# A two-layer hybrid encoder on one core: sums, rows and value projections of the first phase placed differently, more fill ahead of the attention, and the weights' low halves subtracted by GpSimd in that phase

## The chip, the cores and the metric

One NeuronCore of a Trainium2 chip runs the whole kernel. The metric is device time in microseconds (us), the median of three runs. The engines are TensorE (PE in the profile; PEld is its weight load), VectorE (DVE), ScalarE (ACT), GpSimd (POOL) and SyncE (SP, which issues most DMAs). Each engine works through its own instructions in the order in which they were written, and waits on semaphores where it needs another engine's result.

## The reference, cut to what matters

```python
D_MODEL, SEQ, DEPTH, HEAD_DIM = 1024, 512, 2, 64          # batch 1, float32

for l in range(DEPTH):
    hn = rmsnorm(x, norm_mix_g[l])
    proj = hn @ w_in[l]
    (aq, ak, av, bx, by, cq, ck, cv, dq, dk, dv, gl) = jnp.split(proj, split_points, axis=-1)
    ya = mixer_a(aq, ak, av, ...)   # dense attention, 8 query and 2 key heads, q and k normed per head, axial rotary
    yb = mixer_b(bx, by, ...)       # width-4 convolution, two gated linear scans (forward, backward), GeLU gate
    yc = mixer_c(cq, ck, cv, ...)   # attention in a window of +-128, with a sink, rotary
    yd = mixer_d(dq, dk, dv, ...)   # three dilated windows, combined by their softmax denominators, rotary
    gates = sigmoid(gl + gate_bias[l])
    merged = sum(gates[:, :, n] * (y_n @ w_proj_n[l]) for n, y_n in enumerate((ya, yb, yc, yd)))
    x = x + merged @ w_out[l]
    hn = rmsnorm(x, norm_mlp_g[l])
    x = x + square(relu(hn @ w_mlp1[l])) @ w_mlp2[l]
return rmsnorm(x, norm_final_g)
```

## The kernel before, in words

**Weights.** All weights are cut into tiles of 128 x 1024 float32, 158 for each layer, in the order of `PLAN`. A tile is loaded by SP into `raw` (three buffers), ScalarE casts it to a high half `whi` (`whi()`, line 118), and VectorE subtracts: `wlo = raw - whi` (`wlo()`, line 127). Activations are split in the same way (`xh`, `xl`). A float32 product is then three matmuls in the fp32r type: xh by whi, xl by whi, xh by wlo (`mm3`, lines 177 to 179). A group of 128 output channels over all 512 positions takes one tile and 24 matmuls of 512 columns. `ahead` keeps the casts up to three tiles in front of the tile in use, and `lows` puts the subtractions behind each group in VectorE's order.

**First phase** (`phase1`, once a layer). It makes the projections for the mixers, 30 groups in the order of `P1SEQ`: BX and BY (mixer B), K (keys of A and C), AQ, CQ, DQ, DK. Six PSUM banks (tags mm, s, t, two each) take the groups in turn, and one bank, `misc`, takes small sums. Between the groups stand: the column norm (`norm_cols`), its row form (`norm_row`: four small matmuls against the identity, then `bcast_row`: a float32 matmul of a one-row operand with a row of ones, to spread the row over 128 partitions), the sums of squares for the per-head norms (`head_scale`), and a second row of three entries spread through a selector (line 484). `rope` turns pairs of groups: four VectorE products from PSUM (`tt`, line 338), sums (`stk`, `stkf`), and stores to DRAM by SP. Mixer B's element work waits in a queue of closures, `bq`, and `tick` runs some of them behind each group, as `TICKS` says.

**Behind it.** `values_ac` computes the values for A and C: four tiles of 128 positions, 24 matmuls of 256 columns each. Then attention A runs, step by step, mixed with `fill(1)`: the gate logits (GL) and the projection (PR) of mixer B, in pieces of 6 matmuls. `merge(a, b, na, nb, first)` starts with one attention step, then `first` pieces of fill, then spreads the rest in the ratio nb to na. `MG` holds these numbers for A, C and D. `attn_gqa` loads K and Q from DRAM at its start (lines 779, 783); its first two matmuls are lines 796 and 797. Attention C runs mixed with `values_d` (values for D, tiles VD) and more fill; attention D with fill; and `attn_d_end`, which combines the three dilated groups (weights `w12`, spread by the matmuls of line 1100), runs mixed with `FN` pieces of the last fill, with `E1`, `E2` and `E3` empty steps in it. Then come the output projection and the MLP.

Of the kernel before, what the change touches and what calls it, by code (L numbers as in the profile page):

```python
# [40 lines left out]
MG = ((35, 48, 3), (41, 71, 2), (18, 47, 12))  # L41

E1, E2, E3, FN = (1, 5, 2, 15)
# [32 lines left out]
class Body:  # L76
    RAWB, HLB = 3, 3

    def __init__(self, ctx, tc, w, x, vec, tab, cst, out):
        self.tc, self.nc, self.ctx = tc, tc.nc, ctx  # L80
        self.w, self.x, self.vec, self.tab, self.cst, self.out = w, x, vec, tab, cst, out
        pool = lambda n, b=1, **k: ctx.enter_context(tc.tile_pool(name=n, bufs=b, reuse_waits="tile", **k))
        self.cp = pool("cp")
        self.rawp, self.hlp = pool("rawp", self.RAWB), pool("hlp", self.HLB)
        self.xgp = pool("xgp")
        self.sm = pool("sm", 3)
        self.psp = pool("psp", 2, space=PSUM)
# [5 lines left out]
        self.rr = self.held = 0  # L93

# [27 lines left out]
    def wlo(self):  # L122
# [3 lines left out]
        for s in self.parts(i):  # L126
            self.nc.vector.tensor_tensor(out=lo[:, s], in0=raw[:, s], in1=hi[:, s].bitcast(F32), op=ALU.subtract)  # L127
# [45 lines left out]
    def mm3(self, ps, st, mv, n, step=0):  # L173
        mm = self.nc.tensor.matmul
        for k in range(n):
# [4 lines left out]
            if step and k % step == step - 1 and k < n - 1:  # L180
                yield
        self.lows()
# [78 lines left out]
    def norm_row(self, rcol, pool):  # L261
        nc = self.nc
        ps = self.misc()
        for c in range(4):
            nc.tensor.matmul(ps[0:1, c * 128:(c + 1) * 128], rcol[:, c:c + 1], self.ident)
        row = pool.tile([1, S], F32, tag="nrow", name="nrow", bufs=1)
        nc.scalar.copy(row, ps[0:1, :])
        return row

    def bcast_row(self, row, out):  # L270
        nc = self.nc
        ps = self.misc()
        nc.tensor.matmul(ps, self.ones[0:1, :], row)
        nc.scalar.copy(out, ps)
# [110 lines left out]
    def group(self, *key):  # L385
# [4 lines left out]
        self.run(self.proj8(hl, ps))  # L390
# [6 lines left out]
    def phase1(self, l):  # L397
# [15 lines left out]
        self.vD = self.drp.tile([3, S, 256], F32, tag="vD", name="vD")  # L413
        ckp, skp = self.table(4, "b0"), self.table(5, "b1")
        c1, s1 = self.table(0, "c1"), self.table(1, "s1")
        X, sqt = {}, {}
# [3 lines left out]
        def squares(key, Xs, n=128):  # L420
            sqt[key] = []
            for x in Xs:
                sq = p1.tile([128, S], F32, tag="sqq", name="sqq", bufs=2)
                ns.activation(out=sq[0:n], in_=x[0:n], func=AF.Square)
                sqt[key].append(sq)

        def head_scale(key, nh, sel, n=128):

            ps = self.misc()
            for c in range(4):  # L430
                for z in range(2):
# [12 lines left out]
        def q_scale(p):  # L444
            nv.tensor_tensor(
                out=self.rqs[:, :, 4 * p:4 * p + 4], in0=head_scale(p, 4, C_SEL4),
# [3 lines left out]

        X["bx", 0], X["bx", 1] = self.several([("BX", f) for f in range(2)], self.xmv, (1, 2, 3, 4, 6))
# [6 lines left out]
        row = self.norm_row(rcol, p1)  # L458
        X["k", 1] = self.group("K", 1)
        self.bcast_row(row, self.rb)  # L460
# [4 lines left out]
        nc.sync.dma_start(out=rd.rearrange("(o n) -> o n", o=1), in_=row)  # L465
# [6 lines left out]
        yk = head_scale("k", 2, C_SELK, 64)  # L472
# [4 lines left out]
        ps = self.misc()  # L477
        for c in range(4):
            nc.tensor.matmul(ps[0:3, c * 128:(c + 1) * 128], kc[:, c, :], self.ident)
        krow = p1.tile([3, S], F32, tag="krow", name="krow", bufs=1)  # L480
        ns.copy(krow, ps[0:3, :])
# [10 lines left out]
        q_scale(0)  # L492
# [5 lines left out]
        self.gelu_b(0, self.group("BY", 0))  # L498
        q10 = self.group("AQ", 1, 0)
# [3 lines left out]
        q_scale(1)  # L503
        self.rope(q10, q11, T, self.qsA[4:8], True)
        self.gelu_b(2, self.group("BY", 2))
        self.gelu_b(3, self.group("BY", 3))
# [5 lines left out]
        for n, (k, a) in enumerate(QKS):  # L512
# [8 lines left out]
            else:  # L521
                isq = k == "DQ"
                self.rope(x[0], x[1], seq if isq else key, (self.qD if isq else self.kD)[a], False, perm=a > 0)
        self.tick(100)
        nv.tensor_scalar(out=self.rs8p, in0=self.roff, scalar1=0.125, scalar2=None, op0=ALU.mult)

    def values_ac(self):
# [3 lines left out]
        for c in range(4):  # L531
# [10 lines left out]
            )  # L542
    def conv_b(self, l, f, ps):
# [124 lines left out]
    def values_d(self):  # L668
# [462 lines left out]
    def merge(self, a, b, na, nb, first=0):  # L1131
# [8 lines left out]
        step(0)  # L1140
        for _ in range(first):
            step(1)
# [10 lines left out]
    def layer(self, l):  # L1153
# [311 lines left out]
def _tables():  # L1465
# [52 lines left out]
```

## Time and profile before

| what | value |
|---|---|
| median of three runs | 2015.62 us (2018.54, 2015.62, 2010.84) |
| profiled execution, its own time | 2011.35 us |
| its span, first to last instruction | 2009.6 us |
| TensorE busy | 1988.3 us, 99% |
| weight loads busy | 1657.4 us, 82% |
| VectorE busy | 1300.8 us, 65% |
| ScalarE busy | 998.2 us, 50% |
| GpSimd busy | 0.2 us |
| granted TensorE clock, mean | 0.997 |

The time of the profiled execution is 1.75 us longer than its span. A matmul's duration in the profile is longer than its share of the pipeline: a matmul of 512 columns is listed with 0.39 us, but the next starts 0.23 us later, so the pace is read from one start to the next. For the same reason a busy share of 99% says only that TensorE was hardly ever without a matmul in flight.

### The profile page before, as it was taken

How to read it: one execution, taken by the hardware profiler on the slowest of the kernel's cores; microseconds unless marked ns; L12 is line 12 of the kernel's file. 1: busy time of each engine (PE TensorE's matmuls, PEld its weight loads, DVE VectorE, ACT ScalarE, POOL GpSimd, SP SyncE). 2: the span in 40 equal slices, each digit the busy share in tenths (PEclk: the TensorE clock that was granted, in tenths of full speed). 3: DMA queues.
4: the chain of work that ended last, by engine and by line, in shares of the span. 5: the costliest groups of instructions: out<-in, count | busy, mean ns of one | idle time of the engine just before them, and what ended most of it. 6: DMA issues, size and time to landing. Idle time of an engine off the chain costs nothing.

```text
span 2009.6 us, 26003 instructions
## 1 busy us (share of the span) xinstructions
PE 1988.3 (99%) x9752; PEld 1657.4 (82%) x9752; DVE 1300.8 (65%) x2322; ACT 998.2 (50%) x1749; POOL 0.2 (0%) x4
## 2 busy tenths in 40 slices
PE   9999999999999999999999999999999999999998
PEld 7888789888788888888878878898877888888887
DVE  6889775766666544444658897758676655544445
ACT  4357786855734332332323668868566344322322
POOL 0000000000000000000000000000000000000000
PEclk9999999999999999999999999999999999999999
DMA  5454424333443323333335553152353433323231
GB/s 192 145 159 137 131 65 144 116 103 118 114 133 130 95 95 95 105 95 95 134 99 166 157 156 106 44 177 95 105 134 95 163 95 97 103 95 99 91 104 63
DMA packets 91858, 233.35 MB, mean 116 GB/s; under 512 B 16442, under 2 KB 22714, under 8 KB 91732
## 3 DMA queue, kind: packets, MB, share of 16 engines
q1 hardware_dynamic: 88852, 227.49, 36.5%
q10 hardware_dynamic: 2880, 4.20, 0.6%
q8 instruction: 77, 1.26, 0.3%
q14 instruction: 49, 0.40, 0.1%
HBM read 207.38 MB, written 24.27 MB: 115 GB/s over the span
## 4 chain that ended last, share of the span: by engine, by line
PE 93%; DVE 3%; ACT 2%; DMA 1%; issue 1%; SPq 0%; DVEq 0%; ACTq 0%
PE ps_mm L177 14%; PE ps_mm L178 14%; PE ps_mm L179 14%; PE ps_t L177 6%; PE ps_t L179 6%; PE ps_t L178 6%; PE ps_s L177 6%; PE ps_s L178 6%; PE ps_s L179 6%; PE ps_o L856 2%; PE ps_t L835 2%; PE ps_s L796 1%; PE ps_s L797 1%; PE ps_s L946 1%; PE ps_o L1031 1%; PE ps_t L1005 1%
## 5 line engine op out<-in xcount | busy, mean ns | idle before, releaser
L118 ACT CAST whi<-raw 128x1024 fp32r<-128x1024 f32 (+1 forms) x318 | 329.1, 1041 | 302.6 <-PE ps_mm L178 94.1
L127 DVE TENSOR_TENSOR wlo<-raw,whi 128x1024 fp32r<-128x1024 f32 (+1 forms) x318 | 384.7, 1213 | 95.4 <-ACT whi L118 92.5
L177 PE MATMUL ps_mm<-xh,whi 128*128 128x512 f32 x720 | 286.3, 398 | 0.0
L179 PE MATMUL ps_mm<-xh,wlo 128*128 128x512 f32 x720 | 281.7, 391 | 0.0
L178 PE MATMUL ps_mm<-xl,whi 128*128 128x512 f32 x720 | 281.6, 391 | 0.0
L179 PEld LDWEIGHTS ps_mm<-xh,wlo 128*128 128x128 f32 x720 | 135.6, 188 | 29.7
L177 PEld LDWEIGHTS ps_mm<-xh,whi 128*128 128x128 f32 x720 | 135.7, 188 | 27.3 <-issue 0.8
L178 PEld LDWEIGHTS ps_mm<-xl,whi 128*128 128x128 f32 x720 | 135.7, 188 | 26.5
L177 PE MATMUL ps_t<-xh,whi 128*128 128x512 f32 x368 | 143.6, 390 | 0.0
L179 PE MATMUL ps_t<-xh,wlo 128*128 128x512 f32 x368 | 143.3, 389 | 0.3 <-DVE wlo L127 0.3
L178 PE MATMUL ps_t<-xl,whi 128*128 128x512 f32 x368 | 143.2, 389 | 0.0
L177 PE MATMUL ps_s<-xh,whi 128*128 128x512 f32 x352 | 138.5, 394 | 0.0
L179 PE MATMUL ps_s<-xh,wlo 128*128 128x512 f32 x352 | 137.0, 389 | 0.0
L178 PE MATMUL ps_s<-xl,whi 128*128 128x512 f32 x352 | 137.0, 389 | 0.0
L845 DVE TENSOR_TENSOR PT<-ps_t,PT 128x512 fp32r<-128x512 f32 (+2 forms) x128 | 75.1, 586 | 64.0 <-ACT PT L842 59.3
L829 ACT ACTIVATE P<-P,al 128x512 f32<-128x512 f32 (+2 forms) x128 | 82.6, 645 | 16.9 <-DVE al L828 15.7
L842 ACT CAST PT<-ps_t 128x512 fp32r<-128x512 f32 (+2 forms) x128 | 63.8, 500 | 46.7 <-PE ps_o L856 43.2
L177 PEld LDWEIGHTS ps_t<-xh,whi 128*128 128x128 f32 x368 | 69.1, 188 | 17.2 <-issue 3.0
L179 PEld LDWEIGHTS ps_t<-xh,wlo 128*128 128x128 f32 x368 | 69.1, 188 | 15.1 <-DVE wlo L127 0.7
L178 PEld LDWEIGHTS ps_t<-xl,whi 128*128 128x128 f32 x368 | 69.1, 188 | 14.3
L177 PEld LDWEIGHTS ps_s<-xh,whi 128*128 128x128 f32 x352 | 66.1, 188 | 14.8 <-issue 1.4
L178 PEld LDWEIGHTS ps_s<-xl,whi 128*128 128x128 f32 x352 | 66.1, 188 | 14.0 <-issue 0.5
(425 smaller groups left out, 4237.1 us busy)
## 6 DMA issues: line engine op xcount, KB each, us to landing
raw<-in_w_dram SPq DMA_DIRECT2D x314, 512.0 KB, 3.5
Qr<-qD SPq DMA_DIRECT2D x48, 128.0 KB, 3.9
Kd<-kD SPq DMA_DIRECT2D x48, 128.0 KB, 4.0
qsA<-stk SPq DMA_DIRECT2D x32, 128.0 KB, 2.3
qsC<-stk SPq DMA_DIRECT2D x32, 128.0 KB, 2.4
K<-ks SPq DMA_DIRECT2D x16, 256.0 KB, 5.9
Q<-qsA SPq DMA_DIRECT2D x16, 256.0 KB, 4.0
Q<-qsC SPq DMA_DIRECT2D x16, 256.0 KB, 5.2
```

What stands on the lines that cost most here:

```text
L118: self.nc.scalar.copy(hi[:, s], self.raws[i][:, s])
L127: self.nc.vector.tensor_tensor(out=lo[:, s], in0=raw[:, s], in1=hi[:, s].bitcast(F32), op=ALU.subtract)
L177: mm(ps, sh, mh, start=(k == 0), stop=False)
L178: mm(ps, sh, ml, start=False, stop=False)
L179: mm(ps, sl, mh, start=False, stop=(k == n - 1))
L796: nc.tensor.matmul(ps[:, 0:n], qq, Kt[j][:, 0, b0 * 128:b1 * 128], start=True, stop=False)
L797: nc.tensor.matmul(ps[:, 0:n], qq, Kt[j][:, 1, b0 * 128:b1 * 128], start=False, stop=True)
L829: ns.activation(out=P[:, 0:n], in_=P[:, 0:n], func=AF.Copy, scale=ls)
L835: nc.tensor.transpose(pt[:, b * 128:(b + 1) * 128], P[:, b * 128:(b + 1) * 128], self.ident)
L842: ns.copy(st["dst"][0], st["src"])
L845: nv.tensor_tensor(out=st["dst"][1], in0=st["src"], in1=st["dst"][0].bitcast(F32), op=ALU.subtract)
L856: nc.tensor.matmul(o, a, b, start=(n_ == 0), stop=(n_ == len(mm) - 1))
```

## The change

In the first phase (up to the AC values) the subtraction that gives `wlo` is issued to GpSimd; elsewhere it stays on VectorE. The two spread rows are now split in a high part (rows 0 on) and a low part (rows 32 on) and spread by one fp32r matmul each, with a selector built by memsets on GpSimd and a ScalarE copy. The key sums stack both halves of 64 partitions in one tile, so each position block takes one matmul instead of two. Sums and rows are issued inside groups (`within`), behind the fifth of eight steps. `values_ac` moves from the start of attention A to the end of the first phase, before the remaining closures, two of which now run behind each of its four parts. `merge` gets a place (`before`) for the first attention step among the first pieces of fill. `values_d` uses an order of matmuls that needs `wlo` last. `E1` and `FN` go up by one.

```diff
-MG = ((35, 48, 3), (41, 71, 2), (18, 47, 12))
-E1, E2, E3, FN = (1, 5, 2, 15)
+MG = ((35, 48, 5, 4), (41, 71, 2), (18, 47, 12))
+E1, E2, E3, FN = (2, 5, 2, 16)
...
     def wlo(self):
...
-            self.nc.vector.tensor_tensor(out=lo[:, s], in0=raw[:, s], in1=hi[:, s].bitcast(F32), op=ALU.subtract)
+            self.lo_engine.tensor_tensor(out=lo[:, s], in0=raw[:, s], in1=hi[:, s].bitcast(F32), op=ALU.subtract)
...
+    def mm3s(self, ps, st, mv, n, step=0):
+        mm = self.nc.tensor.matmul
+        for k in range(n):
+            (sh, sl), mh = st(k), mv(k)[0]
+            mm(ps, sh, mh, start=(k == 0), stop=False)
+            mm(ps, sl, mh, start=False, stop=False)
+            if step and 4 * k == 3 * n - 4:
+                yield
+        for k in range(n):
+            mm(ps, st(k)[0], mv(k)[1], start=False, stop=(k == n - 1))
+        self.lows()
...
-    def norm_row(self, rcol, pool):
+    def rows(self, cols, n, pool):
+        nc, rw = self.nc, self.rw
+        nc.vector.tensor_copy(rw[:, :, 0:n].bitcast(F32R), cols)
+        nc.vector.tensor_tensor(out=rw[:, :, 32:32 + n], in0=cols, in1=rw[:, :, 0:n], op=ALU.subtract)
         ps = self.misc()
+        m = 32 + n
         for c in range(4):
-            nc.tensor.matmul(ps[0:1, c * 128:(c + 1) * 128], rcol[:, c:c + 1], self.ident)
-        row = pool.tile([1, S], F32, tag="nrow", name="nrow", bufs=1)
-        nc.scalar.copy(row, ps[0:1, :])
+            nc.tensor.matmul(ps[0:m, c * 128:(c + 1) * 128], rw[:, c, 0:m], self.ident)
+        row = pool.tile([m, S], F32R, tag=f"row{n}", name="row", bufs=1)
+        nc.scalar.copy(row, ps[0:m, :])
         return row
-    def bcast_row(self, row, out):
+    def spread_rows(self, row, n, sel):
         ps = self.misc()
-        nc.tensor.matmul(ps, self.ones[0:1, :], row)
-        nc.scalar.copy(out, ps)
+        self.nc.tensor.matmul(ps, self.sel[0:32 + n, sel], row)
+        return ps
...
     def group(self, *key, within=None):
...
-        self.run(self.proj8(hl, ps))
+        for k, _ in enumerate(self.proj8(hl, ps, 1)):
+            if k == 4 and within:
+                within()
...
+        def head_sums(key, nh, sel, c0=0, c1=4):
+            if c0 == 0:
+                SUM[key] = self.misc()
+            sq = sqt[key]
+            for c in range(c0, c1):
+                for z, t in enumerate(sq):
                     nc.tensor.matmul(
-                        ps[:, nh * c:nh * c + nh], sqt[key][z][0:n, c * 128:(c + 1) * 128],
-                        self.cs[0:n, sel:sel + nh], start=(z == 0), stop=(z == 1),
+                        SUM[key][:, nh * c:nh * c + nh], t[:, c * 128:(c + 1) * 128],
+                        self.cs[:, sel:sel + nh], start=(z == 0), stop=(z == len(sq) - 1),
                     )
...
+        self.lo_engine = nc.gpsimd
...
-        X["q", 1] = self.group("AQ", 0, 1)
-        F = self.misc()
-        nc.tensor.matmul(F, self.cs[0:3, C_SEL3:C_SEL3 + 128], krow)
+        X["q", 1] = self.group("AQ", 0, 1, within=lambda: X.update(row=self.rows(kc, 3, p1)))
+        F = self.spread_rows(X["row"], 3, 1)
...
+        self.lo_engine = nc.vector
+        self.values_ac()
         self.tick(100)
...
+            self.tick(2)
...
-                yield from self.paced(last, self.mm3(
+                yield from self.paced(last, self.mm3s(
...
-        step(0)
-        for _ in range(first):
-            step(1)
+        for i in range(first + 1):
+            if i == before:
+                step(0)
+            if i < first:
+                step(1)
```

Three places show what stands where now. The first is TensorE's order where attention A of layer 0 begins: lines 177 to 179 (178 to 180 in the change) on `ps_t` of 256 columns are the last values, lines 796 and 797 (833 and 834) are the first attention step, and `ps_mm` of 512 columns is fill. Before:

```order
L177 MATMUL ps_t<-whi,xh 128x256
L178 MATMUL ps_t<-wlo,xh 128x256
L179 MATMUL ps_t<-whi,xl 128x256
L796 MATMUL ps_s<-K,Q 128x512 [waits DMAHW2_49,DMAHW3_49,DMAHW1_49,DVE_49]
L797 MATMUL ps_s<-K,Q 128x512
L177 MATMUL ps_mm<-xh,whi 128x512 [waits DVE_49,Activation_49]
L178 MATMUL ps_mm<-xl,whi 128x512
```

and now, after the 24 matmuls of the first fill group, of which the last two stand here:

```order
L179 MATMUL ps_mm<-xl,whi 128x512
L180 MATMUL ps_mm<-xh,wlo 128x512
L833 MATMUL ps_s<-K,Q 128x512 [waits DMAHW4_49,DMAHW3_49,DMAHW2_49]
L834 MATMUL ps_s<-K,Q 128x512
L178 MATMUL ps_mm<-xh,whi 128x512 [waits DVE_49,Activation_49]
L179 MATMUL ps_mm<-xl,whi 128x512
L180 MATMUL ps_mm<-xh,wlo 128x512 [waits DVE_49]
L178 MATMUL ps_mm<-xh,whi 128x512
L179 MATMUL ps_mm<-xl,whi 128x512
L180 MATMUL ps_mm<-xh,wlo 128x512
L833 MATMUL ps_s<-K,Q 128x512 [waits PE_49]
```

The first attention step has moved behind 24 matmuls of fill, and the second fill group now begins directly behind it.

The second place is ScalarE's order at the same point: `yB` is mixer B's last product, `VV` the AC values, `whi` the casts for the fill groups behind the first, and `P,al` the exponentials of the first attention step. Before:

```order
L653 CAST yB<-btq 128x512 [waits DVE_49]
L538 ACTIVATE VV<-ps_t,ny 128x4x64 [waits PE_49]
L538 ACTIVATE VV<-ps_mm,ny 128x4x64 [waits PE_49]
L538 ACTIVATE VV<-ps_s,ny 128x4x64 [waits PE_49]
L538 ACTIVATE VV<-ps_t,ny 128x4x64 [waits PE_49]
L118 CAST whi<-raw 128x1024 [waits DMAHW3_49]
L118 CAST whi<-raw 128x1024 [waits DMAHW4_49]
L808 ACT_TABLE_LOAD [waits DMAHW2_49,DMAHW1_49,DMAHW7_49,DMAHW0_49]
L808 ACTIVATE P,al<-ps_s,an,rqs 128x512 [waits DVE_49]
```

and now:

```order
L678 ACTIVATE btq<-btq 128x512 [waits DVE_49] x2
L573 ACTIVATE VV<-ps_s,ny 128x4x64 [waits PE_49]
L573 ACTIVATE VV<-ps_t,ny 128x4x64 [waits PE_49]
L690 CAST yB<-btq 128x512 [waits DVE_49]
L119 CAST whi<-raw 128x1024 [waits DMAHW3_49,Pool_49]
L119 CAST whi<-raw 128x1024 [waits DMAHW4_49,Pool_49]
L119 CAST whi<-raw 128x1024 [waits DMAHW1_49,PE_49,Pool_49]
L757 ACT_TABLE_LOAD
L757 ACTIVATE gt<-gt,d_hb 128x512 [waits DVE_49]
L845 ACTIVATE P,al<-ps_s,an,rqs 128x512 [waits DVE_49]
```

The values are read out among mixer B's closures now, and the casts still stand behind the last of those; a third cast and a gate have come in front of the first exponentials.

The third place is VectorE's order at the rotation of the last query pair of layer 0. Before:

```order
L338 TENSOR_TENSOR tt<-ps_s,s_210 128x512
L127 TENSOR_TENSOR wlo<-raw,whi 128x1024 [waits DMAHW4_49,Activation_49]
L361 TENSOR_TENSOR stkf<-tt 128x512 [waits DMAHW3_49,DMAHW5_49,DMAHW2_49,DVE_49]
L361 TENSOR_TENSOR stkf<-tt 128x512 [waits DVE_49]
L656 TENSOR_TENSOR yB<-btq,yB 128x512
L127 TENSOR_TENSOR wlo<-raw,whi 128x1024 [waits DMAHW5_49,PE_49,Activation_49]
```

and now:

```order
L356 TENSOR_TENSOR tt<-ps_t,c_215 128x512
L356 TENSOR_TENSOR tt<-ps_s,s_217 128x512
L379 TENSOR_TENSOR stkf<-tt 128x512 [waits DMAHW4_49,DMAHW3_49,DMAHW5_49,DMAHW2_49,DVE_49]
L379 TENSOR_TENSOR stkf<-tt 128x512 [waits DVE_49]
L693 TENSOR_TENSOR yB<-btq,yB 128x512 [waits Activation_49]
```

The subtractions are gone from VectorE's order; GpSimd has 33 of them in each layer, one behind the other, with nothing else between them.

## Rows read from the trace of the kernel before

**Rows 1.** The page's first part: busy us, share of the span, instructions.

```profile
PE 1988.3 (99%) x9752; PEld 1657.4 (82%) x9752; DVE 1300.8 (65%) x2322; ACT 998.2 (50%) x1749; POOL 0.2 (0%) x4
```

**Rows 2.** Waits of TensorE: engine, line, releaser, total us, times, longest us.

```profile
PE ps_s L796 <- DMA Q<-qsA: 5.4, 2, 3.2
...
PE ps_misc L1100 <- DVE w L1096: 2.0, 2, 1.0
...
PE ps_mm L178 <- DVE wlo L127: 1.3, 2, 0.6
```

**Rows 3.** TensorE's timeline where attention A begins, both layers (start us, us, instruction).

```profile
205.39 0.28 PE L179 MATMUL ps_t<-whi,xl 128*128 128x256 f32 x1
207.87 0.47 PE L796 MATMUL ps_s<-K,Q 128*128 128x512 f32 x1 [2.20 <-DMA Q<-qsA]
...
1198.58 0.28 PE L179 MATMUL ps_t<-whi,xl 128*128 128x256 f32 x1
1202.03 0.47 PE L796 MATMUL ps_s<-K,Q 128*128 128x512 f32 x1 [3.17 <-DMA Q<-qsA]
```

**Rows 4.** Windows after that wait in layer 1: busy us, PEclk behind POOL.

```profile
1203.40:1206.90 3.50, 3.50 (x11) 2.68 (x10) 3.46 (x7) 3.47 (x4) 0.00 (x0) 0.51 1.03 263
```

**Rows 5.** TensorE's timeline: first matmuls of two groups in succession.

```profile
67.03 0.39 PE L177 MATMUL ps_s<-xh,whi 128*128 128x512 f32 x1
...
72.47 0.39 PE L177 MATMUL ps_t<-xh,whi 128*128 128x512 f32 x1
```

**Rows 6.** ScalarE's and VectorE's timelines where attention A of layer 0 begins.

```profile
210.11 2.01 ACT L118 CAST whi<-raw 128x1024 fp32r<-128x1024 f32 x2
213.43 0.78 ACT L808 ACTIVATE P<-ps_s,an,rqs 128x512 f32<-128x512 f32 x1
...
198.42 2.13 DVE L361 TENSOR_TENSOR stkf<-tt 128x512 f32<-128x512 f32 x2
```

**Rows 7.** Timelines at the D values of layer 0: TensorE, then ScalarE.

```profile
333.02 0.28 PE L177 MATMUL ps_mm<-whi,xh 128*128 128x256 f32 x1
333.93 0.39 PE L178 MATMUL ps_mm<-wlo,xh 128*128 128x256 f32 x1 [0.64 <-DVE wlo L127]
...
331.59 1.98 ACT L118 CAST whi<-raw 128x1024 fp32r<-128x1024 f32 x2
```

**Rows 8.** Timelines at the end of attention D, layer 0: VectorE, then TensorE.

```profile
572.87 0.69 DVE L159 TENSOR_TENSOR yD<-og,yD 128x512 fp32r<-128x512 f32 x1 [0.69 <-ACT yD L158]
...
574.93 0.39 PE L177 MATMUL ps_s<-yD,whi 128*128 128x512 f32 x1
```

**Rows 9.** TensorE's timeline: spread of the norm row, then the key sums.

```profile
32.20 1.12 PE L273 MATMUL ps_misc<-nrow,ones 1*128 1x512 f32 x2
...
38.92 1.94 PE L432 MATMUL ps_misc<-cs,sqq 64*128 64x2 f32 x16
```

**Rows 10.** VectorE's groups, 155 to 172 us: line, operation, count | busy us, mean ns.

```profile
L647 DVE TENSOR_TENSOR_SCAN btq<-bta,btg 128x512 f32<-128x512 f32 x2 | 2.4, 1224 | 0.1
L127 DVE TENSOR_TENSOR wlo<-raw,whi 128x1024 fp32r<-128x1024 f32 x2 | 2.4, 1206 | 0.0
```

**Rows 11.** ScalarE's and TensorE's timelines: a tile's cast, its low half's first use.

```profile
1124.57 2.01 ACT L118 CAST whi<-raw 128x1024 fp32r<-128x1024 f32 x2
1126.94 0.50 PE L179 MATMUL ps_t<-xh,wlo 128*128 128x512 f32 x1 [0.29 <-DVE wlo L127]
...
131.20 2.01 ACT L118 CAST whi<-raw 128x1024 fp32r<-128x1024 f32 x2
134.61 0.39 PE L179 MATMUL ps_t<-xh,wlo 128*128 128x512 f32 x1
...
16.87 3.10 ACT L118 CAST whi<-raw 128x1024 fp32r<-128x1024 f32 x3
20.48 0.40 PE L179 MATMUL ps_mm<-xh,wlo 128*128 128x512 f32 x1
```

**Rows 12.** The windows view of that stretch: us, busy of PE, PEld, DVE, ACT, POOL.

```profile
155.00:172.00 17.00, 17.00 (x76) 14.08 (x75) 16.18 (x23) 12.73 (x18) 0.00 (x0) 1.00 0.58 177
```

More of the change, by code (lines that the diff above doesn't have):

```diff
@@ L383, in tick, with group @@
             self.bq.popleft()()
-    def group(self, *key):
+    def group(self, *key, within=None):
         n = self.n_group
@@ L413, in phase1 @@
         self.vD = self.drp.tile([3, S, 256], F32, tag="vD", name="vD")
+        self.sel = p1.tile([64, 2, 128], F32R, name="sel")
+        self.rw = p1.tile([128, 4, 35], F32, name="rw", padded_shape=[128, 4, 64])
+        nc.gpsimd.memset(self.rw, 0.0)
+        nc.gpsimd.memset(self.sel[0:35, 0].bitcast(F32), 0.0)
+        for z in (0, 32):
+            nc.gpsimd.memset(self.sel[z:z + 1, 0].bitcast(F32), 1.0)
+        ns.copy(self.sel[0:35, 1], self.cs[0:35, C_SEL3:C_SEL3 + 128])
         ckp, skp = self.table(4, "b0"), self.table(5, "b1")
         c1, s1 = self.table(0, "c1"), self.table(1, "s1")
-        X, sqt = {}, {}
+        X, sqt, SUM = {}, {}, {}
         self.l, self.n_group = l, 2
@@ L421, in squares, with head_scale @@
             sqt[key] = []
[L422 to L431, printed above, removed]
+            for z, x in enumerate(Xs):
+                if z == 0 or n == 128:
+                    sq = p1.tile([128, S], F32, tag="sqq", name="sqq", bufs=2)
+                    sqt[key].append(sq)
+                    o = 0
+                else:
+                    o = n
+                ns.activation(out=sq[o:o + n], in_=x[0:n], func=AF.Square)
+        def head_sums(key, nh, sel, c0=0, c1=4):
[4 more added lines that the diff above has]
+                for z, t in enumerate(sq):
                     nc.tensor.matmul(
-                        ps[:, nh * c:nh * c + nh], sqt[key][z][0:n, c * 128:(c + 1) * 128],
-                        self.cs[0:n, sel:sel + nh], start=(z == 0), stop=(z == 1),
-                    )
+                        SUM[key][:, nh * c:nh * c + nh], t[:, c * 128:(c + 1) * 128],
+                        self.cs[:, sel:sel + nh], start=(z == 0), stop=(z == len(sq) - 1),
+                    )
+        def head_scale(key, nh):
+            ps = SUM[key]
             vq = self.smt(4 * nh, f"vq{nh}")
@@ L457, in phase1 @@
         X["k", 0] = self.group("K", 0)
-        row = self.norm_row(rcol, p1)
+        row = self.rows(rows(rcol, 1), 1, p1)
         X["k", 1] = self.group("K", 1)
-        self.bcast_row(row, self.rb)
+        ns.copy(self.rb, self.spread_rows(row, 1, 0))
         if l == 0:
@@ L464, in phase1 @@
         rd = self.drp.tile([S], F32, tag="rd", name="rd")
-        nc.sync.dma_start(out=rd.rearrange("(o n) -> o n", o=1), in_=row)
+        nc.sync.dma_start(out=rd.rearrange("(c p) -> p c", p=128), in_=rcol)
         nc.sync.dma_start(out=self.roff, in_=rd.rearrange("(p r) -> p r", r=4))
@@ L497, in phase1 @@
         self.rope(X["q", 0], X["q", 1], T, self.qsA[0:4], True)
-        self.gelu_b(0, self.group("BY", 0))
-        q10 = self.group("AQ", 1, 0)
+        self.gelu_b(0, self.group("BY", 0, within=lambda: head_sums(0, 4, C_SEL4, 0, 2)))
+        q10 = self.group("AQ", 1, 0, within=lambda: q_scale(0))
         q11 = self.group("AQ", 1, 1)
@@ L1129, in d_weight, with merge @@
             self.nc.sync.dma_start(out=t[64 * a:64 * (a + 1)], in_=wd[r:r + 1, :].to_broadcast([64, S]))
-    def merge(self, a, b, na, nb, first=0):
+    def merge(self, a, b, na, nb, first=0, before=0):
         e = 0
```

26 lines of the change are left out of this document (10 added, 16 removed).

## The prediction, as put on record

> **What bounds the kernel now.** I read the page's busy shares first, then TensorE's waits, then TensorE's timeline from one start to the next. TensorE is in work for 99% of the span [rows 1], and a group of 24 matmuls of 512 columns starts 5.44 us after the one before it, 0.227 us a matmul [rows 5]. So time can be won only where TensorE waits or issues matmuls that are not needed. Its waits are few and short: twice for the first Q of attention A (5.4 us in all), twice for the weights `w12` at the end of attention D (2.0), twice for the low half of the first D-value tile (1.3) [rows 2]. VectorE bounds nothing as a whole, but there are stretches of the first phase where it is nearly full: 16.18 of 17 us [rows 12].
>
> **The change part by part.**
>
> *Fill ahead of attention A.* In layer 0 the last value matmul starts at 205.39 and has 0.12 us, the first score at 207.87: 2.4 us lost; in layer 1 it is 1198.70 to 1202.03, 3.3 us [rows 3]. Behind the longer wait the granted clock is 0.51, the lower of its two levels (1.2 instead of 2.4 GHz), in a window of 3.5 us [rows 4]; at half pace about 1.6 us of work go missing there. Together 7.3 us. The change puts 24 matmuls of fill, 5.44 us, in front of the first score, so Q may land where it does now with 3.0 and 2.1 us to spare. What is late next: the second fill group now starts at 5.9 us behind the values (5.44 and two scores), and its low half is wanted at 6.35. The casts behind the first group end their first half at 211.1 today, 5.6 us behind the values [rows 6], and the subtraction adds 1.2 us: 6.9, some 0.5 us late. VectorE is quicker to this point by the subtractions that left it, and slower by four value readouts that now stand among mixer B's closures; I let these cancel. Then the third score needs the first exponentials done. They end at 214.2 today, 8.7 us behind the values [rows 6]; two subtractions, 2.4 us, and a gate now stand in front of the row maximum on VectorE, of which I count 1.8 us as new (an estimate), so 10.5, against 9.6 at which TensorE arrives: 0.9 us. I take 1.4 us of new waits in each layer (bounds 0 and 3.6, which would undo the gain): 7.3 - 2.8 = 4.5 us won.
>
> *D values.* The second matmul starts 0.91 us behind the first instead of 0.12 [rows 7], so 0.8 us in each layer. `mm3s` asks for the low half only behind 16 matmuls of high halves, 1.9 us later; the second tile's high half, which is now wanted first, is cast by 333.57 [rows 7], before the ninth matmul at 333.97. 1.6 us won.
>
> *End of attention D.* One more empty step puts one more piece of fill, 6 matmuls or 1.36 us, in front of the matmuls that wait 1.0 us in each layer [rows 2]: 2.0 us won. What is late next is the second half of `yD`: ready at 573.56, wanted at 574.93 [rows 8]; of these 1.4 us the change uses 1.0, so it stays covered.
>
> *Spread rows and key sums.* A spread is two instructions of together 1.12 us [rows 9]; as one fp32r matmul of 512 columns it is 0.23. Two in each layer: 4 x 0.89 = 3.6 us. The key sums are 16 instructions in 1.94 us [rows 9]; half of them go: 2 x 0.97 = 1.9. The query sums are cut in two pieces; a break costs between nothing and 0.2 us, and I take 0.3 for all. The small row matmuls keep their number. In the second row TensorE has 9 matmuls, 2.0 us, between the transposes and the spread, for a ScalarE copy; if that copy meets a cast of 1.0 us it still fits, and I count nothing. 5.2 us won.
>
> *Low halves on GpSimd.* 33 in each layer. VectorE is relieved of about 40 us a layer, but it is not what TensorE waits for in the first phase, so I count that at nothing. What counts is whether GpSimd delivers in time. No row shows such an instruction there. The nearest is VectorE's own, 1.21 us; the slowest pace of any row is the scan, 1.22 us for 512 elements, so 2.45 for 1024 [rows 10]. I take 3.0, nearer to the scan, since this instruction reads two streams and may stand half a microsecond behind a VectorE instruction; the upper end is 4.9, twice the scan. With 0.1 us for the handover, the time from the end of the cast to the first use must be longer than this. The tightest are the first DK tile of layer 1 (cast ends 1125.6, use 1126.94: 1.3 us, and TensorE waits there already), the same in layer 0 (132.25 to 134.61: 2.35) and the first K tile (17.9 to 20.48: 2.6) [rows 11]. At 3.0 these lose 1.8, 0.75 and 0.5: 3.1 us. At 1.2 nothing; at 4.9 these three lose 8.8, and I allow half as much again for the next ones: 13.
> The Trainium skill (GPSIMD Engine Reference, 3.1) gives 4497 ns for a float32 tensor_tensor of 2048 elements on GpSimd, so by estimate 2.25 us for 1024. No row shows it; with it the loss would be 1.1 us and the sum 2.0 us better.
>
> Sum: 4.5 + 1.6 + 2.0 + 5.2 = 13.3 won, 3.1 lost: 10.2 us. The profiled execution took 2011.35 us; it would take 2001.2. The median of the runs shown is 4.3 us above that execution, so the forecast against it is 2015.62 - 10.2 = 2005.4, say 2005.
>
> **The rivals.**
>
> *VectorE and GpSimd hold each other up; about no change.* From 155 to 172 us VectorE is busy for 16.18 us [rows 12], 13.8 without its two subtractions [rows 10]. GpSimd wants 2.45 us in every 5.44, 0.45 of the time. If the two never worked at once, the stretch would need 13.8 + 7.7 = 21.5 us and VectorE would fall 4.5 us behind in each layer. That shows as later rotations, casts and values at the start of attention A, where I have no slack left: up to 9 us, by half of it some 4.5. Result 2010, up to 2014. For it: the stretch is full, and a GpSimd instruction at the scan's pace is twice as long as the longest of VectorE's there. Against it: products that read PSUM make up a good part of the stretch, and the phase has emptier stretches to catch up.
> The Trainium skill (SBUF — State Buffer, Who interferes with whom) has the rule that would do this: a VectorE instruction with two SBUF inputs and a GpSimd instruction that reads SBUF lock each other out for a whole instruction. GpSimd does nothing here before the change, so no row shows it; by that rule VectorE would fall behind in this stretch, without it it would not.
>
> *GpSimd paces the first phase; slower.* Its 33 tiles must come between 17.9 us (the first cast) and 205.5, one every 5.7 us. If one takes 4.9 us and a wait for a scan in front, 6.1 in all, TensorE gets its tiles at that pace: 33 x 0.4 = 13 us a layer, and the tight tiles at the start, 9 or so, 35 in both layers. Less 13.3 won: 2037. It decides from about 4.9 us a tile, where the tight tiles eat the whole gain. Against it stands that this is twice the slowest pace in the trace.
>
> *More fill only moves the wait.* If the second fill group and the third score lose what the first gains, the 4.5 us go and 5.7 stay: 2010.
>
> **How the numbers follow.** The forecast 0.50, the lock 0.25, the pacing 0.15, the moved wait 0.10. The likeliest case alone runs from 1998 (no new waits at GpSimd or at the attention, 16 us won) to 2012. The range over all: 1997 to 2020; it leaves out most of the pacing. 0.5% (10 us) is about what a measurement of this kernel can tell from no change. Faster by more: 0.40 of the forecast's 0.50 and 0.03 each of the lock and the moved wait, 0.46. Within: 0.10 + 0.20 + 0.07 = 0.37. Slower: all of the pacing and 0.02 of the lock, 0.17.
>
> **What would show it.** In the profile of the changed kernel: no wait for Q in front of the first scores, and there a clock of 1.00; waits of 0.5 to 1 us at the second fill group or the third score; none on the D-value low halves nor in front of the `w12` matmuls; spreads as one matmul of 0.4 us. On POOL, 66 subtractions with starts that lie 2 to 3 us apart where they follow directly; waits of TensorE for POOL only at the first DK and K tiles. I am wrong if VectorE's instructions grow longer beside GpSimd, if TensorE waits for POOL at many tiles, or if the last rotation of the phase ends later than it does now.

## The result: slower, 2032 us

The changed kernel takes 2032.35 us (median of 5 executions, 2029.87 to 2033.54); the kernel before, run beside it on the same chip, 2013.17 us (2010.71 to 2018.54). The ratio is 1.0088, with a 95% interval from 1.0073 to 1.0103: slower by 0.9%, 19 us, where 10 us were forecast to be won. The profiled execution took 2031.66 us, with a span of 2029.9 us.

### The profile page after: what moved, and what is told of

Its sections match the earlier page's. It is cut to its first block, busy times and chain, and to the rows that moved or that the text cites. A ratio compares the mean times of both kernels' runs of the same rounds, so it can differ in the third digit from the quotient of the medians.

```text
span 2029.9 us, 26022 instructions
## 1 busy us (share of the span) xinstructions
PE 1991.8 (98%) x9732; PEld 1658.1 (82%) x9732; DVE 1318.1 (65%) x2264; ACT 999.4 (49%) x1751; POOL 172.9 (9%) x78
## 4 chain that ended last, share of the span: by engine, by line
PE 81%; DVE 12%; ACT 3%; issue 2%; DMA 1%; POOL 0%; SPq 0%; DVEq 0%; ACTq 0%; POOLq 0%
PE ps_mm L178 11%; PE ps_mm L180 11%; PE ps_mm L179 11%; PE ps_t L178 5%; PE ps_t L179 5%; PE ps_t L180 5%; PE ps_s L178 5%; PE ps_s L180 5%; PE ps_s L179 5%; PE ps_o L893 2%; PE ps_t L872 2%; DVE tt L356 2%; DVE stkf L379 2%; PE ps_s L833 1%; PE ps_s L834 1%
## 5 line engine op out<-in xcount | busy, mean ns | idle before, releaser
L128 DVE TENSOR_TENSOR wlo<-raw,whi 128x1024 fp32r<-128x1024 f32 (+1 forms) x252 | 304.9, 1212 | 61.3 <-ACT whi L119 58.7
L128 POOL TENSOR_TENSOR wlo<-raw,whi 128x1024 fp32r<-128x1024 f32 x66 | 171.2, 2606 | 231.7 <-ACT whi L119 228.6
```

The lines of the kernel that those rows point to most:

```text
L128: self.lo_engine.tensor_tensor(out=lo[:, s], in0=raw[:, s], in1=hi[:, s].bitcast(F32), op=ALU.subtract)
```

## The profile after

First the busy shares, which answer to [rows 1].

```profile
PE 1991.8 (98%) x9732; PEld 1658.1 (82%) x9732; DVE 1318.1 (65%) x2264; ACT 999.4 (49%) x1751; POOL 172.9 (9%) x78
```

VectorE lost 66 subtractions, some 80 us of work, and yet it is busy for 17 us more than before. That is the line to stop at: its other instructions must have grown. The next groups are VectorE's in the first phase of layer 0, from 16 to 206 us (line, operation, tiles, shapes, count | busy us, mean ns), in the changed kernel:

```profile
L379 DVE TENSOR_TENSOR stkf<-tt 128x512 f32<-128x512 f32 x10 | 20.2, 2058 | 0.0
L596 DVE SCALAR_TENSOR_TENSOR xc<-bx,ve,xc 128x512 f32<-128x512 f32 x12 | 13.0, 1084 | 0.5 <-ACT xc L594 0.3
L362 DVE TENSOR_TENSOR tt<-tt 128x512 f32<-128x512 f32 x10 | 11.2, 1159 | 0.0
L672 DVE SCALAR_TENSOR_TENSOR btq<-btg,btq 128x512 f32<-128x512 f32 x6 | 8.0, 1325 | 5.5 <-ACT btg L666 5.5
L530 DVE TENSOR_SCALAR Tq<-b,ve 128x512 f32<-128x512 f32 x4 | 3.4, 908 | 0.8 <-DMA b<-in_tab_dram 0.8
L356 DVE TENSOR_TENSOR tt<-ps_s,c 128x512 f32<-128x512 f32 x5 | 3.4, 678 | 0.0
```

And the same groups where the low halves stay on VectorE (the first experiment, `first_alone`):

```profile
L379 DVE TENSOR_TENSOR stkf<-tt 128x512 f32<-128x512 f32 x12 | 10.9, 953 | 0.0
L596 DVE SCALAR_TENSOR_TENSOR xc<-bx,ve,xc 128x512 f32<-128x512 f32 x12 | 9.0, 749 | 0.2
L362 DVE TENSOR_TENSOR tt<-tt 128x512 f32<-128x512 f32 x10 | 6.4, 685 | 0.0
L672 DVE SCALAR_TENSOR_TENSOR btq<-btg,btq 128x512 f32<-128x512 f32 x8 | 5.5, 690 | 0.7 <-ACT btg L666 0.7
L530 DVE TENSOR_SCALAR Tq<-b,ve 128x512 f32<-128x512 f32 x4 | 1.8, 482 | 1.5 <-DMA b<-in_tab_dram 1.5
L356 DVE TENSOR_TENSOR tt<-ps_s,c 128x512 f32<-128x512 f32 x5 | 3.4, 683 | 0.0
```

Instructions that read two SBUF tiles take 1.4 to 2.2 times as long in the mean, and `Tq`, which reads one SBUF tile and a scalar, 1.9 times; the one that reads PSUM (`tt<-ps_s,c`) did not change. GpSimd's own timeline, and VectorE's beside it, show how (start us, us; the rows of POOL name two and three subtractions in a row):

```profile
155.69 5.22 POOL L128 TENSOR_TENSOR wlo<-raw,whi 128x1024 fp32r<-128x1024 f32 x2 [4.95 <-ACT whi L119]
...
199.76 8.84 POOL L128 TENSOR_TENSOR wlo<-raw,whi 128x1024 fp32r<-128x1024 f32 x3 [8.59 <-ACT whi L119]
```

```profile
155.72 0.68 DVE L356 TENSOR_TENSOR tt<-ps_t,sk 128x512 f32<-128x512 f32 x1
156.31 5.15 DVE L379 TENSOR_TENSOR stkf<-tt 128x512 f32<-128x512 f32 x2
161.39 0.68 DVE L693 TENSOR_TENSOR yB<-btq,yB 128x512 fp32r<-128x512 f32 x1
...
199.80 0.68 DVE L356 TENSOR_TENSOR tt<-ps_s,s 128x512 f32<-128x512 f32 x1
200.39 5.93 DVE L379 TENSOR_TENSOR stkf<-tt 128x512 f32<-128x512 f32 x2
206.25 2.91 DVE L693 TENSOR_TENSOR yB<-btq,yB 128x512 fp32r<-128x512 f32 x1
```

The engines take turns (the lock of the prediction's first rival). GpSimd's first subtraction ends at 158.10 and VectorE's first `stkf` product 0.55 us later; GpSimd's second ends at 160.91, VectorE's second product again 0.56 us later. From 199.8 to 209.1 it goes so three times, and two `stkf` products and one `yB` product, which need 2.6 us, take 8.8. The `tt` products beside them read PSUM and run at 0.68 us. Over all VectorE instructions that overlap a subtraction, the time above the median of the same form without overlap comes to 44.3 us in layer 0 and 39.3 in layer 1 (forms that never stand free of a subtraction are left out): as much as the 39.8 us a layer that were taken off VectorE. A subtraction itself took 2.37 to 2.42 us in 43 of 66 cases and up to 4.84 in the others, 2.61 in the mean. The windows view of the stretch of [rows 12] now reads 16.97 of 17 us for VectorE, with less work done in it:

```profile
155.00:172.00 17.00, 17.00 (x76) 14.08 (x75) 16.97 (x19) 12.28 (x16) 7.74 (x4) 1.00 0.39 114
```

What that does to TensorE stands in its waits (answering to [rows 2]):

```profile
PE ps_mm L178 <- ACT btg L655: 7.0, 4, 2.0
PE ps_t L179 <- POOL wlo L128: 4.6, 2, 3.1
PE ps_s L833 <- DMA Q<-qsA: 4.5, 1, 4.5
PE ps_t L180 <- POOL wlo L128: 2.6, 2, 1.3
...
PE ps_misc L283 <- issue: 1.7, 1, 1.7
...
PE ps_misc L1137 <- DVE w L1133: 1.2, 2, 0.6
...
PE ps_misc L283 <- DVE rw L279: 1.1, 1, 1.1
...
PE ps_mm L180 <- POOL wlo L128: 0.5, 1, 0.5
```

7.7 us are waits for GpSimd's tiles themselves (VAC, the tiles of the AC values, 4.6; DK00, the first DK tile, 2.6; K0 0.5). The rest stands behind a late VectorE: the gates' PSUM readouts (7.0, none of size before), the rows (1.7 and 1.1, and 0.6 that is not among these lines), and Q in layer 0. The gates' readouts wait because ScalarE does them in order, behind work that waits for VectorE:

```profile
170.24 0.63 ACT L678 ACTIVATE btq<-btq 128x512 f32<-128x512 f32 x1 [3.07 <-DVE btq L672]
...
174.28 0.69 ACT L655 ACTIVATE btg<-ps_mm,d_lgb 128x512 f32<-128x512 f32 x1
...
178.12 0.62 ACT L690 CAST yB<-btq 128x512 fp32r<-128x512 f32 x1 [2.57 <-DVE btq L689]
178.64 0.68 ACT L655 ACTIVATE btg<-ps_mm,d_lgb 128x512 f32<-128x512 f32 x1
```

The changed kernel and `first_alone` issue the same 9732 matmuls in the same order, so their starts can be compared one by one. The lag of the changed kernel grows by 8.2 us at the gates, 4.4 at the first scores of layer 0, 3.5 at the rows and 13.0 at GpSimd's tiles (8.0 of these at VAC); with 0.6 won back in attention A of layer 1 it ends at 28.4 us.

In layer 0 the last rotation is stored at 213.62 instead of 200.58 us; the values' matmuls end at 215, so the 5.4 us of fill in front of the first score no longer reach:

```profile
225.62 0.67 PE L833 MATMUL ps_s<-K,Q 128*128 128x512 f32 x1 [4.50 <-DMA Q<-qsA]
```

Behind this wait the granted clock is 0.55, near the lower of its two levels, from 226.0 to 229.5 us, and in layer 1 it is 0.50 from 1210 to 1214, behind the wait for VAC; the prediction wanted 1.00 at the first scores, which `first_alone` has.

The other steps hold. The spread is one instruction of 0.50 us instead of [rows 9]'s two, the key sums are 8 instead of 16:

```profile
35.18 0.50 PE L291 MATMUL ps_misc<-row,sel 33*128 33x512 f32 x1
41.16 0.95 PE L466 MATMUL ps_misc<-cs,sqq 128*128 128x2 f32 x8
```

The D values start without the wait of [rows 7]. The wait for `w12` is 1.2 us in all instead of 2.0 and has not gone.

## Experiments

Times are medians; ratios are to the kernel before, run on the same chip beside the kernel.

**Which part costs?** `first_alone`: the one line `self.lo_engine = nc.gpsimd` becomes `nc.vector`. `low_alone`: the kernel before, with GpSimd as `lo_engine` in the first phase and nothing else.

> The low halves of the first phase stay on VectorE; all the rest of the change stands. Theory (lock): what the new GpSimd work does to VectorE makes the whole loss, so this kernel shows the first part's gain: about 13 us under the kernel before, near 2000 us, VectorE's stkf products back at about 0.95 us a piece (2.06 in the changed kernel), and no new wait at the gates. Rival (first part): the moved sums and values themselves set VectorE back, and the time stays above the kernel before. Rival (smaller terms): the first part gains 5 us or less.

> The kernel before, with only the 33 low halves of each layer's first phase moved to GpSimd. Theory (lock): 20 to 30 us slower than the kernel before, since here too VectorE loses about 40 us a layer in blocked instructions, and the values wait at the end of the phase. Rival (the loss comes from the combination, late lows before the earlier values): under 10 us slower.

`first_alone` 2003.74 us, ratio 0.9953 [0.9940, 0.9966]; `low_alone` 2044.41 us, 1.0149 [1.0130, 1.0168]. GpSimd's part alone costs 30 us; on top of the first part it costs 27 (from the two ratios). The first part of the change (all but GpSimd) wins 9.5 us, or 8.7 by the medians, not 13.

**Reading, or any work of GpSimd?** In both kernels VectorE keeps its subtractions, and TensorE waits for nothing of GpSimd's. Behind each low half:

```
+            self.nc.gpsimd.tensor_tensor(out=self.idle, in0=raw, in1=hi.bitcast(F32), op=ALU.subtract)   # idle_read
...
+            self.nc.gpsimd.tensor_copy(self.idle[:, 0:1], hi[:, 0:1].bitcast(F32))                       # idle_write
+            for _ in range(2):
+                self.nc.gpsimd.memset(self.idle.bitcast(F32), 0.0)
```

> Low halves on VectorE; beside each of the 33, GpSimd does the same subtraction once more into a tile that nobody reads before it is overwritten. TensorE never waits for GpSimd here. Theory (lock): VectorE keeps its 40 us of subtractions and loses about as much again in blocked instructions, so it falls far behind in the dense part of the phase: 25 us or more above first_alone. Rival (late delivery): only tiles that GpSimd delivers late cost time; here it delivers none, so within 4 us of first_alone.

> As idle_read, but GpSimd copies one column of the high half (so that it starts at the same moment) and then fills the same tile twice with zeros: it writes 128x1024 twice and reads next to nothing. Theory (lock by reading): VectorE's instructions stay as long as in first_alone, the time within 4 us of first_alone. Rival (any GpSimd work beside VectorE slows it): as slow as idle_read.

`idle_read` 2107.20 us, 1.0469 [1.0452, 1.0487]: 103 us above `first_alone`, though TensorE waits for nothing that GpSimd makes. The 103 us are not the price of the lock alone: VectorE keeps its own subtractions here and delivers them late, 14 weight loads wait up to 2.2 us until GpSimd has read their buffer, and the granted clock is 0.978 in the mean, not 0.998. `idle_write` 2009.82 us, 0.9981 [0.9971, 0.9990]. VectorE's groups, first of `idle_read`, then of `idle_write`, 16 to 206 us:

```profile
L128 DVE TENSOR_TENSOR wlo<-raw,whi 128x1024 fp32r<-128x1024 f32 x27 | 49.5, 1843 | 8.6 <-ACT whi L119 8.6
L598 DVE SCALAR_TENSOR_TENSOR xc<-bx,ve,xc 128x512 f32<-128x512 f32 x12 | 15.2, 1263 | 0.2
L532 DVE TENSOR_SCALAR Tq<-b,ve 128x512 f32<-128x512 f32 x4 | 3.5, 940 | 0.8 <-DMA b<-in_tab_dram 0.8
```

```profile
L128 DVE TENSOR_TENSOR wlo<-raw,whi 128x1024 fp32r<-128x1024 f32 x33 | 39.9, 1218 | 9.7 <-ACT whi L119 9.7
L600 DVE SCALAR_TENSOR_TENSOR xc<-bx,ve,xc 128x512 f32<-128x512 f32 x12 | 9.0, 749 | 0.2
L534 DVE TENSOR_SCALAR Tq<-b,ve 128x512 f32<-128x512 f32 x4 | 2.9, 780 | 1.0 <-DMA b<-in_tab_dram 1.0
```

Instructions with two SBUF inputs grow only beside a GpSimd that reads (`wlo` 1843 ns against 1218 in `idle_write` and 1219 in `first_alone`). The 6 us of `idle_write` (2 more than expected) have another form: its fills hold up VectorE's instructions with one SBUF input and a scalar (`Tq` 780 ns instead of 482), and the row and two low halves come late. That these lengthened instructions make them late is not shown.

**Lock or late tiles?** Three kernels choose which of the 33 tiles a layer go to GpSimd (`j` is the tile's place in the layer), one cuts the subtraction in four.

```
+        eng = self.lo_engine if j not in (2, 3, 21, 32, 33, 34) else self.nc.vector   # tight_on_vector
...
+        eng = self.lo_engine if j < 13 else self.nc.vector                            # early_only
...
+        eng = self.lo_engine if j > 23 else self.nc.vector                            # late_only
...
+        n = 4 if self.lo_engine is self.nc.gpsimd else 1                              # quarters
+        cuts = [slice(p * (1024 // n), (p + 1) * (1024 // n)) for p in range(n)] if n > 1 else self.parts(i)
+        for s in cuts:
```

> The changed kernel with 27 of the 33 low halves a layer on GpSimd; VectorE keeps the ones whose use follows their cast soonest (K 0 and 1, the first DK tile) and those in front of attention A (VAC, first GL). Theory (lock): only the waits for GpSimd's own tiles go (7.7 us in the changed kernel's trace), so 5 to 10 us better than the changed kernel, 2022 to 2028. Rival (late delivery, the sum of the prediction): nearly the whole loss goes, within 5 us of first_alone (2004).

> The changed kernel with GpSimd taking only 11 tiles a layer, K 0 to BY 2, in the first 75 us of the phase, where VectorE has room. Theory (lock, with the price where VectorE is full): under a third of the loss, 2004 to 2011. Rival (each blocked instruction costs the same anywhere): a third of 28 us, 2013. Rival (late delivery): the K tiles have short gaps, and the waits for K and for the rows stay; 2008.

> The changed kernel with GpSimd taking only the last 11 tiles a layer, from the second DQ1 tile to the first GL tile, where VectorE is busy for 31 of 32 us. Theory (lock, with the price where VectorE is full): more than half of the loss, 2018 to 2028, with the waits at the gates and for Q in front of attention A as in the changed kernel. Rival (each blocked instruction costs the same anywhere): 2013. Rival (late delivery): only the VAC and GL tiles are near their use, under 2010.

> The changed kernel with each GpSimd subtraction cut into four of 256 columns. Lock for a whole instruction: VectorE's longest block falls from about 2.2 us to about 0.6, but GpSimd asks for the same columns, so VectorE's lost time falls by less than half and the kernel stays 10 us or more above first_alone, 2014 to 2028. Rival (the loss comes from the length of a single block): nearly all of it goes, under 2010. Rival (a fixed cost of each GpSimd instruction counts): slower than the changed kernel.

| kernel | median us | ratio, 95% interval | above `first_alone` |
|---|---|---|---|
| `tight_on_vector` | 2023.14 | 1.0051 [1.0036, 1.0066] | 19 |
| `early_only` | 2007.96 | 0.9974 [0.9964, 0.9984] | 4 |
| `late_only` | 2022.28 | 1.0041 [1.0027, 1.0055] | 19 |
| `quarters` | 2021.44 | 1.0041 [1.0027, 1.0056] | 18 |

With the tight tiles back on VectorE two thirds of the loss stay, and so do the gates' waits (the low half of a VAC tile comes 1.8 us late from VectorE too); the same waits come back from the last 11 tiles alone. Waits of `tight_on_vector`, then of `late_only`:

```profile
PE ps_mm L180 <- ACT btg L657: 6.5, 4, 2.0
```

```profile
PE ps_mm L180 <- ACT btg L657: 6.5, 4, 2.0
PE ps_s L835 <- DMA Q<-qsA: 5.8, 2, 2.9
```

Eleven tiles cost 4 us where VectorE has room (busy for 44 of 58 us in `first_alone`) and 19 where it is full (62 of 64). Against the medians of `first_alone`, VectorE's instructions beside them are lengthened by 14.2 and 11.6 us (layer 0 and 1) in `early_only`, by 20.3 and 21.4 in `late_only`: 1.6 times as much, for more than four times the loss. So the blocked time alone does not give the price; who waits for VectorE there does. Cut in four, GpSimd needs 0.97 us a piece, 3.9 a tile, so its own tiles come later (4.2 us of waits for VAC), and VectorE still loses 36.8 and 35.2 us (48.3 and 43.6 in the changed kernel, against the same medians of `first_alone`).

`early_no_k` leaves the K tiles out of `early_only` (`4 < j < 13`); with them the tile BX 2 (`j` = 4) goes back to VectorE, so that GpSimd's eight tiles run from the first AQ tile to BY 2.

> early_only without the K tiles: GpSimd takes 8 tiles a layer, BX 2 to BY 2. Theory (the 4 us of early_only are the waits behind K, where VectorE's blocked copy of the row and GpSimd's K 0 tile are late): within 2 us of first_alone, so GpSimd's work is free here, and gains nothing either. Rival (any GpSimd subtraction costs): 2 us or more above first_alone.

2005.27 us, 0.9963 [0.9951, 0.9976]: 1.5 to 2 us above `first_alone`, of which 1.1 is the wait for the row of layer 0. So GpSimd's work is nearly free there, and wins nothing.

**Where did 4 us of the first part go?** `fill_back` sets `MG[0]` back to `(35, 48, 3)`, `values_back` moves `values_ac()` back behind `next(attn)`, `both_back` does both, all from `first_alone`.

> first_alone with the order in attention A back as before: the first score ahead of all fill, three pieces behind it; the values stay at the end of the phase. Theory: the waits behind PT (0.46 and 0.70 us) in each layer go, the wait for Q comes back and is longer than before, since the weight load still stands in front of Q: 4 to 6 us in layer 0, 3 to 4 in layer 1, with a lower clock behind it; some 3 to 7 us slower than first_alone. Rival (the fill in front wins nothing net): within 1 us of first_alone.

> first_alone with the values of attentions A and C computed where the kernel before has them, behind the loads of K and Q; the fill in front of the first score stays. Theory (the move of the values put a weight load in front of K and Q, and Q came late by it): Q lands in time, no wait for it, but that weight then comes late to the third fill tile and to ScalarE's exponentials as in load_held (2 and 4 us at the third score); 2006 to 2011. Rival (the move of the values costs nothing): as first_alone, 2004.

> first_alone with both edits at the start of attention A undone (values behind the loads of K and Q, the first score ahead of all fill); the rows, the key sums, the D values and the end of attention D stay changed. By the stalls of the traces these four are worth about 6.5 us, so 2005.5 to 2006.5 (theory: the two edits win 1 to 2 us together, far less than the 4.5 of the prediction, since new waits eat most of it). Rival (the fill in front is worth what was predicted, 4.5 us): 2008 or more. Rival (the two edits together lose): under 2003.

| | first score ahead of the fill | fill ahead of the first score |
|---|---|---|
| values behind the loads of K, Q | `both_back` 2005.05, 0.9953 [0.9939, 0.9968] | `values_back` 2010.72, 0.9987 [0.9978, 0.9996] |
| values in the first phase | `fill_back` 2013.75, 0.9995 [0.9986, 1.0004] | `first_alone` 2003.74, 0.9953 [0.9940, 0.9966] |

Each edit alone loses 6 to 9 us (`fill_back` is 8.5 to 10 us slower than `first_alone`, where 3 to 7 were expected); together they win nothing that these intervals can tell from zero (1.3 us by the medians, 3.2 by the profiled spans). The DMA queue shows why the values' move costs: in `first_alone` the second line here, a load of 512 KB for a weight tile, stands in front of K and Q.

```profile
198.64 1.74 SPq L381 DMA_DIRECT2D kD<-stkf  x4
200.48 0.40 SPq L103 DMA_DIRECT2D raw<-in_w_dram  x1
200.97 1.32 SPq L816 DMA_DIRECT2D K<-ks  x2
202.35 1.54 SPq L820 DMA_DIRECT2D Q<-qsA  x3
```

The same stretch of the kernel before:

```profile
200.58 1.75 SPq L363 DMA_DIRECT2D kD<-stkf  x4
202.43 1.33 SPq L779 DMA_DIRECT2D K<-ks  x2
203.80 1.54 SPq L783 DMA_DIRECT2D Q<-qsA  x3
205.39 1.24 SPq L779 DMA_DIRECT2D K<-ks  x2
206.72 0.54 SPq L102 DMA_DIRECT2D raw<-in_w_dram  x1
```

Q is issued 1.45 us earlier and yet comes later: the first score starts at 210.25 in `first_alone`, behind a wait of 1.08 us for Q, and at 207.87 before [rows 3]. In `fill_back` nothing hides it:

```profile
209.33 0.76 PE L833 MATMUL ps_s<-K,Q 128*128 128x512 f32 x1 [5.52 <-DMA Q<-qsA]
...
1205.17 0.76 PE L833 MATMUL ps_s<-K,Q 128*128 128x512 f32 x1 [7.08 <-DMA Q<-qsA]
```

`load_held` issues that load behind K's and Q's; `load_held_w12` also moves the added empty step of attention D's end between the `w12` chain and its matmuls (E1 back to 1, a second `yield` behind the chain); `load_held_w12_mg34` spreads the fill over 34 steps.

```
- while self.n_load < min(self.n_lo + self.RAWB, n):
+ while not self.hold and self.n_load < min(self.n_lo + self.RAWB, n):
...
+ self.hold = True
  self.values_ac()
...
  next(attn)
+ self.hold = False
+ while self.n_load < self.n_lo + self.RAWB:
+     self.wload()
```

> first_alone, whose first score in layer 0 still waits 1.25 us for Q, although 5.44 us of fill now stand in front of it: there the 512 KB load of a weight tile stands in the DMA queue in front of the loads of K and Q, where the kernel before has it behind the third Q. Here that load is issued behind the loads of K and Q. Theory (the load in front makes Q late): Q lands about 2 us earlier, no wait for Q is left in layer 0, 1 to 1.5 us faster than first_alone, unless the low half of the second or third fill tile is late in its place (0.5 to 1.5 us back). Rival (Q is late by the last rotation on VectorE): the wait for Q stays at 1 us or more.

> load_held, with the added empty step of attention D's end between the chain for w12 and the matmuls that read it, and not ahead of the chain (where the casts of the fill piece went in front of the chain's exponentials on ScalarE, and the wait fell from 1.15 to only 0.75 us). Theory: the whole added piece of 1.36 us covers the wait, which goes: 2 x 0.75 us, some 1.5 us faster than load_held. Rival (ScalarE and VectorE are late for another reason): the wait stays above 0.4 us.

> load_held_w12, with the 43 pieces of fill that are left in attention A spread over 34 of its 35 steps. Theory (the change's two pieces more in front leave too little fill between a transposition and the product that reads it, 0.46 and 0.70 us at two places in each layer): these waits go or move, gain up to 2.5 us. Rival (the places just move): no difference, within 1 us.

2010.97, 2009.71 and 2010.82 us; 0.9983 [0.9975, 0.9992], 0.9977 [0.9968, 0.9986], 0.9986 [0.9977, 0.9994]. In `load_held` no wait for Q is left, as expected; yet it is 6 to 7 us slower than `first_alone`, where 1 to 1.5 us less were expected. The held weight is then late itself, ScalarE waits for it in front of its cast, and the third score waits for the exponentials queued behind the cast (layer 1, TensorE, then ScalarE):

```profile
1211.08 0.79 PE L834 MATMUL ps_s<-K,Q 128*128 128x512 f32 x1 [3.78 <-ACT P L846]
...
1207.19 1.04 ACT L120 CAST whi<-raw 128x1024 fp32r<-128x1024 f32 x1 [3.26 <-DMA raw<-in_w_dram]
```

K, Q and the weight want the same transfer time: from 206 to 214 us of `first_alone` the DMA engines are busy throughout, at 233 to 253 GB/s. The order only chooses who waits. With the step behind the chain the wait for `w12` is gone from `load_held_w12`'s list. Spreading the fill only moved the waits for PT (the transposed exponentials).

`first_alone_w12` is `first_alone` with that step moved.

> first_alone with the added empty step of attention D's end between the chain for w12 and the matmuls that read it, as in load_held_w12. Theory: the wait of 0.75 us a layer goes, 1.5 us faster than first_alone, 2002. Rival: the second half of yD is late instead, no gain.

2002.80 us (2002.43 to 2003.12), 0.9950 [0.9936, 0.9964]: the fastest kernel here, 10 us under the kernel before by its ratio and 28 to 30 under the changed one; against `first_alone` the 1 us is not told apart by the times, but the wait for `w12` is gone from the trace.

## Why the prediction was wrong

*The step that failed: "VectorE is relieved of about 40 us a layer, but it is not what TensorE waits for in the first phase, so I count that at nothing."* There was no relief: VectorE lost 44.3 and 39.3 us in blocked instructions. And VectorE does set the end of the phase, through ScalarE's order (gates), the stores of the rotations (Q) and the rows. The lock was named as a rival, with a chance of 0.25 and up to 4.5 us a layer; that price was taken from one stretch of 17 us, and the delay grew over the whole dense part instead: the last rotation of layer 0 comes 13 us later than before, and TensorE loses 16.3 us to `first_alone` in layer 0 and 12.1 in layer 1. `idle_read` against `idle_write` shows the lock, `tight_on_vector` that two thirds of the loss stay when VectorE makes the tight tiles itself, `late_only` where they arise. Two of the prediction's three signs of being wrong came, longer VectorE instructions and a later last rotation; the third did not, since TensorE waits 0.5 us or more for GpSimd at only five tiles.

The Trainium skill (SBUF — State Buffer, Who interferes with whom) says that a VectorE instruction with two SBUF inputs and a GpSimd instruction that reads SBUF exclude each other for a whole instruction, that a GpSimd instruction which only writes does not do this to it, and that a VectorE tensor_scalar in a two-port mode contends with any GpSimd instruction. The traces agree: `stkf` 2058 against 953 ns; `xc` 749 in `idle_write` as in `first_alone`; `Tq`, with one input, 908 beside reads and 780 beside writes, against 482 (in which mode it ran, no trace shows). By that rule the lock should have been the forecast.

*GpSimd's delivery.* The working price of 3.0 us for a tile was near: 2.61. TensorE waits 7.7 us for its tiles, 3.1 were taken; DK00 and K0 as named (2.6 and 0.5), and VAC (4.6), which was not: it stands behind other GpSimd work that the lock had lengthened (8.84 us for three tiles). Giving the tight tiles back won 7.5 us by the ratios, 9 by the medians. That part of the loss is late delivery, and the pacing rival is wrong all the same: GpSimd was busy for 83 of 190 us.

*Fill ahead of attention A,* 4.5 us taken, 0 to 3 measured. The step that failed here is "Q may land where it does now": the moved values put a weight's load in front of Q. The waits at the third score (0.5 and 0.6 us) and at the low half of the second fill tile (0.7 in layer 1) came much as priced; two waits of 0.46 and 0.70 us for PT later in each layer were not foreseen. With Q's wait of 1.08 us in layer 0 they eat most of the gain; that the fill in front wins anything is not shown. The moved-wait rival was nearer here.

*End of attention D,* 2.0 us taken, 0.8 measured: the added piece of fill brought its casts on ScalarE in front of the chain's exponentials. In layer 0 of `first_alone` the cast starts at 550.07 us and the exponentials at 551.03; in `first_alone_w12` the exponentials start at 550.58, ahead of the cast at 550.89, and the wait is gone. The step was right, its place wrong.

*D values and sums,* 6.8 us taken. The D-value waits are gone (1.6 us). By starts on TensorE the four spreads win 2.5 us, not 3.6: the next matmul starts 1.05 us after a spread of the kernel before (the 1.12 of [rows 9] is a duration) and 0.43, not 0.23, after a new one. The key sums win 2.1, with 1.9 taken. `both_back`, which has only these and the end of attention D, is 8 to 9.5 us faster than the kernel before by its times, with 8.8 taken for the three; but the pieces found in the traces come to 7.0 and the profiled spans differ by 4.9, so that the agreement is partly luck.

*A sum.* The lower end of the likeliest case, 1998, does not follow from 16 us won, which gives 1999.5; nothing rests on it.

## What to carry to other kernels

Before work is moved to GpSimd, count what VectorE does beside it: here each VectorE instruction with two SBUF inputs, the scan included, took turns with GpSimd instructions that read SBUF, so 2.4 us subtractions can take back from VectorE all that they took off it. Read how full VectorE is where they fall, and who waits there; the engine's share of the whole span tells nothing of that. When a piece of work moves ahead of loads, read its own loads in the queue: they move too.

## What the runs showed of the chip

- A GpSimd subtraction of 128x1024 float32 takes 2.37 to 2.42 us when nothing blocks it (43 of 66); a quarter of it 0.97 us with the lock (0.72 at least).
- Even VectorE's instructions on 128x16 elements wait for its end: 174 ns alone, 2.0 to 2.4 us when they start just behind a subtraction's start.
- VectorE's scan (two SBUF inputs) takes part: where it starts first it stays at 1.22 us and the subtraction that meets it takes 2.94 to 2.96 in the changed kernel; in `quarters`, where it starts second, it takes 1.64 to 1.65.
- A GpSimd copy of a single column (at least 183 ns) took 1.15 to 1.18 us in 19 of 66 cases, and 2.26 in one, beside VectorE's instructions with two SBUF inputs: the lock holds in both directions.
